# A hybrid encoder layer on one core: the delta rule's block inverses spread over two steps, and gate weights prepared in two parts

## The chip, the cores and the metric

The kernel runs on 1 core of one Trainium2 chip. The metric is the device time of one execution in microseconds (us), here the median of three runs.

## The reference, cut to what matters

One encoder layer: x + RMSNorm(W_out([A | B | M] * silu(z))), where the attention branch A, the delta-rule branch B, the memory branch M and the gates z all read one input projection of RMSNorm(x) (sequence 2048, width 1024). The change lies in branch B and in the projection of the gates.

```python
def gated_delta_rule_chunked(q, k, v, g, beta):      # per head and direction, chunks of 64
    ...
    lower = jnp.where(strict, jnp.einsum('...id,...jd->...ij', k_beta, k) * decay, 0.0)
    t_mat = lower + jnp.eye(CHUNK, dtype=lower.dtype)
    sol = lax.linalg.triangular_solve(t_mat, rhs, left_side=True, lower=True, unit_diagonal=True)
    ...
    def step(state, inp):
        qc, kc, uc, wc, ac, dc = inp
        v_new = uc - jnp.einsum('...cd,...de->...ce', wc, state)
        o = jnp.einsum('...cd,...de->...ce', qc, state) + jnp.einsum('...ij,...je->...ie', ac, v_new)
        state = state * dc[..., None, None] + jnp.einsum('...cd,...ce->...de', kc, v_new)
        return state, o
```

Four heads, forward and backward; the two directions are summed.

## The kernel before, in words

The kernel works on chunks of 128 tokens (16 of them, `TB`) and on two pairs of heads (`hp`); a step of the recurrence takes chunk s forward and chunk 15 - s backward for both heads of a pair, so there are 32 steps. TensorE (PE) runs the stage in the order in which the program writes it (`pin(T)`); VectorE (DVE), ScalarE (ACT), GpSimd (POOL) and the DMA queue of SyncE (SP) are ordered by a planner with a clock of its own, and each then serves its queue in that order.

Between the products of the delta rule the program puts gate products: `fill(n)` issues n products of 128x512 of `all_units`, which works through ten groups of 192 products (gates `z` and memory queries `mq`, 24 products to one output tile). There are 1920 of them in all; 48 come before the stage, 72 are kept for the attention's start (`START`), and a last `fill` issues what is left. `FILL` holds the numbers: entries 4 to 10 are those inside one step (18 in sum), entry 3 the ones between the parts of a head and between the parts of the last `finish`, entry 1 those of each chunk of the preparation (`s3a`), entry 2 those behind each of the two block inverses.

Each group needs its weights: `load_w` (L165) starts their DMA on POOL's queue, has ACT sum the squares (`wss`), DVE add them (`wsb`), PE sum over partitions (`norm_pow2`, L150), and then DVE, ACT and POOL make the scaled halves `wparts`. `all_units` calls it for the next group at the third output tile (k == 2) of a group.

The preparation writes, for each chunk, the matrices `NI` (products of `kq` with itself times decays), and then inverts the 32x32 diagonal blocks on DVE into `FT`. `inverse(hp, s)` builds the 128x128 inverse `F` of one chunk from them, in five parts with a `yield` between: part 0 loads `nt` (`n<-NI`) and `ft` and copies blocks to `F` and `Tb`; part 1 computes `zz` and its copy `zs`; part 2 `to` and `fo`, copied to `Tb` and `F`; part 3 `z2` and its copy `z2s`; part 4 `f2`, copied to `F`. In the trace `zz`, `fo`, `z2` and `f2` are one tile, `inv`, and `to` is `invt`.

`step` (L985) runs, on PE: `ks`, `qp`, then part 1 of the inverse of chunk s+1, 2 gate products, `tx` (with `F` of this chunk), 2 products, part 2, a part of the `finish` of the pair before, 6 products, `kv`, part 3, `av`, 6 products, part 4, 2 products. DVE makes `vn` from `tx` and the state `St` from `kv`; ACT makes `oo` from `qp`. The first chunk of each pair has its parts 0 to 3 run ahead of the pair's steps (the head), with 30 + 3 x 12 products between. `finish` scales, turns and gates the outputs of a pair, two chunks at a time; for the first pair it rides in the second's steps, for the second it runs at the end, with 12 products after each of its parts.

Working buffers of the stage: two `F`, one each of `Tb`, `nt`, `ft` and `oo`, two of `xx`; four PSUM buffers under the tag `tp`.

Of the kernel before, what the change touches and what calls it, by code (L numbers as in the profile page):

```python
# [11 lines left out]
F32 = mybir.dt.float32  # L12
# [20 lines left out]
LAG = 5  # L33
FILL = (72, 10, 216, 12, 0, 2, 2, 6, 0, 6, 2, 40, 0)


@with_exitstack
def hybrid_layer(ctx: ExitStack, tc: tile.TileContext, t: dict, out, dbg=None):
# [126 lines left out]
    def load_w(srcs, width, fac=(1.0,), fetch=None):  # L165


        n = wcount[0]
        wcount[0] += 1
# [14 lines left out]
        sb, y, e, sc = small("wsb", BF16), small("wy"), small("we", I32), small("wsc")  # L184
        V.tensor_tensor(sb, ss[0], ss[1], op=ALU.add)
        norm_pow2(f"{n}", sb, sc, y, e)
        cs = [small("wc1", bufs=2)] * (len(fac) - 1) + [small("wc0", pool=const)]
# [6 lines left out]
        G.tensor_tensor(parts[1][:, 1], raws[1], parts[1][:, 0], op=ALU.subtract)  # L194
        return [(w[:, 0], w[:, 1]) for w in parts], cs

# [63 lines left out]

    def load_group(segs, fetch=None, fac=(1.0,)):
# [6 lines left out]
        return load_w(src, sum(n for _, n in segs), fac, fetch)  # L268

    def tok_proj(ps, wg, tb):  # L270
# [265 lines left out]
    def z_load(pair):  # L536
        wg, (c, half) = load_group([(3600 + 256 * pair, 256)], fac=(1.0, 0.5))
        V.tensor_scalar(gate_cs[pair], c, vcs15 if pair < 4 else wd if pair < 6 else mvcs15, None, op0=ALU.mult)
        return wg, half

# [4 lines left out]
    with tc.tile_pool(name="s2", bufs=1) as p:  # L545
        wg, bcs, xbs, svs, kts_ = {0: nxt[0]}, {0: nxt[1]}, {}, {}, {}

        def b_proj(ch, b):
            g, u = ch // 2, ch % 2
            if u == 1 and b == 0:  # L550
                if g < 5:
                    wg[g + 1], bcs[g + 1] = load_group([(1536 + 256 * (g + 1), 256)])
                else:
                    wg[6] = z_load(4)
            if b == 0:
# [131 lines left out]
    def all_units():  # L687
# [3 lines left out]
        def load(kind, n):  # L691
            if kind == "z":
                return z_load(n)
            wg, (c,) = load_group([(3088 + 256 * n, 256)], fac=(SCALE * 2.0 ** 30,))
            V.tensor_scalar(mcs[:, 2 * n:2 * n + 2], c.to_broadcast([128, 2]), mkcs, None, op0=ALU.mult)
            return wg
# [222 lines left out]
    with tc.tile_pool(name="s3b", bufs=1) as p:  # L919
        Fb = [p.tile([128, 2, 2, 128], F32, tag=f"F{i}", name=f"F{i}") for i in range(2)]  # L920
        Tb = p.tile([128, 2, 64], F32, tag="T64", name="T64")
        for i in range(2):
            G.memset(Fb[i], 0.0)
        G.memset(Tb, 0.0)

# [5 lines left out]
        def inverse(hp, s):  # L931

            nm = f"{hp}_{s}"
# [16 lines left out]
            zz = ps[:, 0:64].rearrange("p (h i) -> p h i", h=2)  # L950
            fo = ps[:, 64:128].rearrange("p (h i) -> p h i", h=2)
            to = tp_ps(f"invt{nm}", (128, 2, 32))
            z2 = ps[:, 192:320].rearrange("p (h i) -> p h i", h=2)
            f2 = ps[:, 320:448].rearrange("p (h i) -> p h i", h=2)
# [30 lines left out]

        def step(hp, s, St, oss, inv, inv1, side):
            nm = f"{hp}_{s}"
            cc = (s, TB - 1 - s)
            sh = [128, 2, 2, 128]
            F = Fb[s % 2]  # L990
            xx = p.tile([128, 2, 4, 2, 128], F32, tag="xx", name=f"xx{nm}", bufs=2)
# [15 lines left out]
            fill(FILL[4])  # L1007
            oo = p.tile(sh, F32, tag="oo", name=f"oo{nm}")
            if s > 0:
# [13 lines left out]
            fill(FILL[6])  # L1023
            next(inv1, None)
            side()
# [19 lines left out]
            fill(FILL[9])  # L1045
            next(inv1, None)
            fill(FILL[10])
# [13 lines left out]
        def finish(hp, oss):  # L1061
# [6 lines left out]
            for c in range(0, TB, 2):  # L1068
                tags = ("oo", "vn") if hp and c % 4 else ("fi", "ga")
                oi = p.tile([128, 2, 2, 128], F32, tag=tags[0], name=f"fi{hp}_{c}")  # L1070
                ga = p.tile([128, 2, 256], F32, tag=tags[1], name=f"ga{hp}_{c}")
# [14 lines left out]
        done = iter(())  # L1086
        for hp in range(2):
            St = p.tile([128, 2, 2, 128], F32, tag="St", name=f"St{hp}")
            oss = p.tile([128, 2, TB], F32, tag="oss", name=f"oss{hp}", bufs=2)
            inv = inverse(hp, 0)  # L1090
            next(inv)
            fill(30)
            for _ in range(3):
                next(inv)
                fill(FILL[3])
            for s in range(TB):
                inv1 = inverse(hp, s + 1) if s + 1 < TB else iter(())
                next(inv1, None)
                step(hp, s, St, oss, inv, inv1, lambda: next(done, None))
                inv = inv1  # L1100
            done = finish(hp, oss)
        fill(24)
        for _ in done:
            fill(FILL[3])

# [451 lines left out]
```

## Time and profile before

| | |
|---|---|
| median of 3 runs | 2458.18 us (2453.1 to 2463.39) |
| the profiled execution | 2451.84 us |
| its span, first to last instruction | 2450.1 us |
| mean granted clock of TensorE | 0.987 |
| PE busy | 2320.4 us (95%) |
| DVE busy | 1652.8 us (67%) |
| ACT busy | 1302.7 us (53%) |
| POOL busy | 750.2 us (31%) |

Times in the profile count from the first instruction; a row of a list of waits names the engine that waited, what it was about to do, and after the arrow the engine and tile that it waited for. PE's matmuls are pipelined, so that a busy PE is not one at its peak. The preparation of the delta rule lies between about 650 and 900 us, the steps between about 905 and 1277, the last `finish` up to 1330.

### The profile page before, as it was taken

Reading aid. Unit: us, or ns where it says so; the run is one execution under the profiler, and the core shown is the slowest. Engines: PE = TensorE matmul, PEld = TensorE weight load, DVE = VectorE, ACT = ScalarE, POOL = GpSimd, SP = SyncE. Lnnn points to the kernel's source line nnn. Section 1 sums busy time; section 2 is a strip of 40 time slices with the busy share of each in tenths; the row PEclk is TensorE's granted clock in tenths of the full one; section 3 lists DMA queues with packets and bytes.
Section 4 is the critical chain, followed back from the end, with each engine's and each line's share of the span. In section 5 each row is a group of like instructions: output and inputs, shape, how many; then the busy total and the mean of one; then the engine's idle time right before and its main releaser. Section 6 shows DMA issues by size and latency. Waiting matters only on the chain.

```text
span 2450.1 us, 42346 instructions
## 1 busy us (share of the span) xinstructions
PE 2320.4 (95%) x15846; PEld 1463.9 (60%) x15846; DVE 1652.8 (67%) x3321; ACT 1302.7 (53%) x2516; POOL 750.2 (31%) x446
## 2 busy tenths in 40 slices
PE   6999999999999989999999999999999999899998
PEld 6888864455454446656664566666666666544443
DVE  7777659999658845545553777878887777355553
ACT  5634436544443135555553788888988878211110
POOL 2146432112112221121020444444555645122110
PEclk9999999999999999999999999999999999999999
DMA  6456555334477457767865999999999999676551
GB/s 224 142 133 148 122 120 179 115 108 124 132 247 240 115 171 208 226 196 231 241 211 177 226 234 242 240 244 236 247 240 236 239 227 222 195 249 195 183 166 67
DMA packets 942126, 471.59 MB, mean 192 GB/s; under 512 B 721952, under 2 KB 889440, under 8 KB 941664
## 3 DMA queue, kind: packets, MB, share of 16 engines
q1 hardware_dynamic: 929472, 425.88, 67.8%
q0 software_dynamic: 12448, 43.00, 5.2%
q8 instruction: 125, 2.05, 0.3%
q14 instruction: 81, 0.66, 0.1%
HBM read 207.59 MB, written 108.10 MB: 129 GB/s over the span
## 4 chain that ended last, share of the span: by engine, by line
PE 34%; DMA 10%; issue 4%; ACT 3%; POOL 2%; DVE 2%; SPq 0%; ACTq 0%; DVEq 0%; POOLq 0%
PE o L51 12%; PE sa L51 8%; PE pva L51 7%; DMA PT<-hla 5%; PE z L51 3%; POOL hla L51 2%; DMA xx<-bx 1%; DMA Od<-oo 1%; ACT Pa L51 1%; PE sm L51 1%; PE pvm L51 1%; ACT hla L51 0%; DMA wor<-in_w_out 0%; DVE hla L51 0%; PE o_last L51 0%
## 5 line engine op out<-in xcount | busy, mean ns | idle before, releaser
L51 PEld LDWEIGHTS <-wparts 128*128 128x128 f16 x3072 | 294.7, 99 | 327.6 <-issue 18.5
L51 POOL TENSOR_TENSOR hla<-Pa,hla 128x1281 f16<-128x1281 f32 x128 | 335.9, 2624 | 309.3 <-DVE hla L51 300.7
L51 DVE TENSOR_REDUCE mxa<-sa 128x1 f32<-128x1024 f32 x256 | 313.3, 1224 | 144.2 <-PE sa L51 143.9
L51 PE MATMUL sa<-K,qa 128*128 128x512 f16 x1536 | 375.3, 381 | 31.3 <-ACT Pa L51 29.3
L51 PE MATMUL pva<-PT,V 128*128 128x256 f16 x3072 | 376.4, 273 | 0.0
L51 PE MATMUL z<-hT,wparts 128*128 128x512 f16 x1536 | 373.4, 384 | 0.0
L51 PEld LDWEIGHTS <-V 128*128 128x128 f16 x3072 | 300.6, 98 | 84.9
L51 ACT ACTIVATE Pa<-sa,mxa,misc 128x1024 f32<-128x1024 f32 x256 | 305.9, 1198 | 57.4 <-DVE mxa L51 55.5
L51 PE MATMUL o<-wo,mhl 128*128 128x512 f16 x1416 | 308.8, 381 | 7.4 <-ACT mhl L51 4.9
L51 ACT CAST hla<-Pa 128x2048 f16<-128x2048 f32 x128 | 243.0, 1899 | 66.8 <-DMA PT<-hla 61.1
L51 PE MATMUL b<-hT,wparts 128*128 128x512 f16 x1152 | 258.2, 381 | 0.0
L51 PEld LDWEIGHTS <-mhl 128*128 128x128 f16 x1464 | 143.6, 98 | 182.4 <-ACT mhl L51 5.2
L51 PEld LDWEIGHTS <-qa 128*128 128x128 f16 x1536 | 150.6, 98 | 167.8 <-issue 39.0
L51 PEld LDWEIGHTS <-hT 128*128 128x128 f16 x2304 | 225.9, 98 | 40.0 <-DVE t L51 9.4
L51 PE MATMUL q<-wparts,hT 128*128 128x256 f16 x1920 | 213.6, 275 | 8.8 <-DVE t L51 8.8
L51 POOL TENSOR_SCALAR wraw<-wraw,wsc 128x1024 f32<-128x1024 f32 (+1 forms) x22 | 76.0, 3454 | 313.1 <-DVE wy L51 269.8
L51 DVE SCALAR_TENSOR_TENSOR y<-xb,convw,y 128x512 f32<-128x512 f32 x192 | 147.8, 782 | 2.0
L77 POOL DMA_DIRECT2D gate<-zg x64 | 35.6, 556 | 367.2 <-DVE zg L51 196.4
L51 ACT CAST mhl<-mr 128x2048 f16<-128x2048 f32 (+1 forms) x16 | 29.1, 1818 | 222.0 <-PE o L51 172.3
L51 DVE SCALAR_TENSOR_TENSOR hla<-Pa,hla 128x768 f16<-128x768 f32 x128 | 135.8, 1061 | 3.4 <-ACT hla L51 3.0
L51 POOL TENSOR_TENSOR mg<-mg 128x1536 f32<-128x1536 f32 (+1 forms) x16 | 55.0, 3437 | 236.1 <-DMA mg<-r 180.8
L51 DVE TENSOR_TENSOR mhl<-mr,mhl 128x2048 f16<-128x2048 f32 (+1 forms) x16 | 46.2, 2887 | 87.5 <-ACT mhl L51 87.5
(358 smaller groups left out, 3211.4 us busy)
## 6 DMA issues: line engine op xcount, KB each, us to landing
xx<-bx SPq DMA_DIRECT2D x64, 512.0 KB
wraw<-in_w_in POOLq DMA_DIRECT2D x42, 512.0 KB, 5.4
wor<-in_w_out SPq DMA_DIRECT2D x32, 512.0 KB
gate<-zg POOLq DMA_DIRECT2D x64, 256.0 KB, 3.9
NI<-nit SPq DMA_DIRECT2D x32, 512.0 KB
mr<-mix SPq DMA_DIRECT2D x13, 1024.0 KB
mg<-r SPq DMA_DIRECT2D x13, 768.0 KB
x<-in_x SPq DMA_DIRECT2D x16, 512.0 KB
```

The costliest lines, as they stand in the source:

```text
L51: ins = f(*args, **kw)
L77: nc.gpsimd.dma_start(to, of)
```

## The change

- The block inverses: part 0, 1 and 2 of chunk n+2 and parts 3 and 4 of chunk n+1 now run in step n. Part 1 comes where part 2 was (behind `tx`), part 2 where part 4 was (end of the step), part 3 where part 1 was (behind `qp`), part 4 where part 3 was (behind `kv`). Steps are counted through both pairs, so the second pair has no head of its own; the first head runs parts 0 to 2 for two chunks and part 3 for one.
- Buffers: three `F`, two `Tb`, two each of `nt`, `ft` and `oo`, three `kq`. The PSUM tiles of the inverse are five short ones in place of two.
- `FILL`: 2 products behind `ks` (were 0), 5 ahead of `tx` (were 2), 23 in a step (were 18); 6 between the parts of the head (were 12); 8 after each part of the last `finish` (new entry 13; were 12). The total of 1920 stays.
- Weights: `load_w` yields ahead of `norm_pow2`; `all_units` calls the first half at k == 1 and the second at k == 4. Earlier stages call both halves at once.

```diff
-FILL = (72, 10, 216, 12, 0, 2, 2, 6, 0, 6, 2, 40, 0)
+FILL = (72, 10, 216, 6, 2, 5, 2, 6, 0, 6, 2, 40, 0, 8)
...
         V.tensor_tensor(sb, ss[0], ss[1], op=ALU.add)
+        yield
         norm_pow2(f"{n}", sb, sc, y, e)
...
-                if k == 2 and not last:
-                    nxt = load(*plan[i + 1])
+                if k in (1, 4) and not last:
+                    if k == 1:
+                        steps = load(*plan[i + 1])
+                    nxt = next(steps)
...
-                kq = p.tile([128, 2, 2, 128], F32, tag="kq", name=f"kq{nm}", bufs=2)
+                kq = p.tile([128, 2, 2, 128], F32, tag="kq", name=f"kq{nm}", bufs=3)
...
-            F = Fb[s % 2]
-            nt = p.tile([128, 2, 2, 128], F32, tag="nt", name=f"n2{nm}")
-            ft = p.tile([128, 2, 2, 2, 32], F32, tag="ft", name=f"ft{nm}")
+            F, Tb = Fb[n % 3], Tbs[n % 2]
+            nt = p.tile([128, 2, 2, 128], F32, tag="nt", name=f"n2{nm}", bufs=2)
+            ft = p.tile([128, 2, 2, 2, 32], F32, tag="ft", name=f"ft{nm}", bufs=2)
...
-            ps = tp_ps(f"inv{nm}", (128, 512))
...
+            zz = tp_ps(f"invz{nm}", (128, 2, 32))
...
+            to, fo = tp_ps(f"invt{nm}", (128, 2, 32)), tp_ps(f"invf{nm}", (128, 2, 32))
...
+            z2 = tp_ps(f"invy{nm}", (128, 2, 64))
...
+            f2 = tp_ps(f"inv{nm}", (128, 2, 64))
...
-            oo = p.tile(sh, F32, tag="oo", name=f"oo{nm}")
+            oo = p.tile(sh, F32, tag="oo", name=f"oo{nm}", bufs=2)
...
             fill(FILL[6])
-            next(inv1, None)
+            next(inv2, None)
...
             fill(FILL[9])
-            next(inv1, None)
+            next(inv2, None)
...
+        order = [(hp, s) for hp in range(2) for s in range(TB)]
+        invs = [inverse(*x) for x in order]
+        for n in range(2):
+            next(invs[n])
+        fill(30)
+        for k in range(3):
+            for n in range(2 if k < 2 else 1):
+                next(invs[n])
+            fill(FILL[3])
+        invs += [iter(()), iter(())]
+        for n, (hp, s) in enumerate(order):
...
+            next(invs[n + 2], None)
+            step(hp, s, St, oss, *invs[n:n + 3], lambda: next(done, None))
+            if s == TB - 1:
+                done = finish(hp, oss)
         fill(24)
         for _ in done:
-            fill(FILL[3])
+            fill(FILL[13])
```

## Rows read from the trace of the kernel before

**Rows 1.** Stretches: window, its length, busy us per engine (count), PEclk, DMA share, GB/s

```profile
core 0: us, PE busy (x) PEld busy (x) DVE busy (x) ACT busy (x) POOL busy (x), PEclk, DMA share, GB/s
905.00:1277.00 372.00, 346.12 (x3658) 243.29 (x3657) 199.56 (x632) 206.35 (x786) 56.97 (x54) 1.00 0.72 217
1277.00:1330.00 53.00, 53.00 (x263) 26.15 (x262) 15.88 (x41) 17.14 (x49) 6.78 (x11) 1.00 0.57 183
```

**Rows 2.** PE's waits, 905 to 1277 us: total us, times, longest

```profile
PE inv L51 <- ACT F L51: 7.2, 9, 1.4
PE inv L51 <- ACT z2s L51: 6.4, 9, 2.0
PE inv L51 <- DMA n<-NI: 5.0, 5, 1.9
PE tx L51 <- DVE xx L51: 1.8, 3, 1.0
PE kv L51 <- DVE vn L51: 1.8, 4, 1.0
```

**Rows 3.** PE's waits over the whole span, the two of the preparation

```profile
PE pg L51 <- DMA kq<-bx: 8.2, 5, 3.2
PE wss L51 <- DVE wsb L51: 8.2, 2, 6.0
```

**Rows 4.** One step in order of time: start, us, engine, operation, count [idle before <- releaser]

```profile
1009.88 1.16 PE L51 MATMUL kv<-vn,xx 128*128 128x128 f32 x8
1010.11 1.14 ACT L51 ACTIVATE oo<-qp,gam 128x128 f32<-128x128 f32 x4 [3.30 <-DMA Od<-oo]
...
1011.13 0.83 ACT L51 COPY F<-inv 32x64 f32<-32x64 f32 x4
...
1012.02 0.45 PE L51 MATMUL inv<-T,n 64*64 64x64 f32 x8 [0.97 <-ACT F L51]
...
1013.39 1.46 PE L51 MATMUL z<-hT,wparts 128*128 128x512 f16 x6
...
1016.49 1.06 PE L51 MATMUL qp<-St,xx 128*128 128x128 f32 x8
...
1020.16 0.48 DVE L51 TENSOR_SCALAR xx<-xx,tail 128x128 f32<-128x128 f32 x2 [2.19 <-DMA xx<-bx]
```

**Rows 5.** The preparation in order of time: two loads of `kq` and a late product

```profile
701.46 0.64 SPq L51 DMA_DIRECT2D kq<-bx  x1
...
704.93 0.48 SPq L51 DMA_DIRECT2D kq<-bx  x1
...
710.18 2.04 PE L51 MATMUL pg<-kq 128*128 128x256 f32 x4 [3.12 <-DMA kq<-bx]
```

**Rows 6.** Stretches behind PE's three longest waits; the granted clock is the third-last column

```profile
712.00:730.00 18.00, 18.00 (x75) 9.24 (x74) 7.77 (x22) 6.50 (x22) 1.10 (x2) 0.89 0.63 209
868.00:880.00 12.00, 12.00 (x45) 4.88 (x44) 9.79 (x24) 2.06 (x2) 4.05 (x4) 0.79 0.58 140
1150.00:1200.00 50.00, 47.21 (x493) 34.39 (x492) 26.02 (x82) 25.97 (x99) 3.19 (x5) 0.97 0.78 240
```

**Rows 7.** The last `finish` in order of time

```profile
1292.50 5.34 PE L51 MATMUL z<-hT,wparts 128*128 128x512 f16 x24
...
1292.70 0.69 DVE L51 SCALAR_TENSOR_TENSOR ga<-ot,ga 128x512 f32<-128x512 f32 x1 [3.57 <-PE ot L51]
...
1293.42 0.36 SPq L51 DMA_DIRECT2D mix<-ga  x1
...
1296.81 0.36 SPq L51 DMA_DIRECT2D ga<-gate  x1
...
1298.32 0.69 DVE L51 SCALAR_TENSOR_TENSOR ga<-ot,ga 128x512 f32<-128x512 f32 x1 [4.33 <-PE ot L51]
```

**Rows 8.** Instructions on the tile `St`: duration min/median/max in ns

```profile
L51 DVE SCALAR_TENSOR_TENSOR St<-St,egl,kv x112: 337/342/349, 923.0 to 1268.6; 128x128 f32<-128x128 f32 x112
```

**Rows 9.** A gate weight during the block inverses, in order of time

```profile
818.31 0.18 PE L51 MATMUL wss<-wsb,onesb 128*128 128x1 bf16 x1 [2.12 <-DVE wsb L51]
...
834.83 2.22 POOL L51 TENSOR_TENSOR wparts<-wraw,wparts 128x1024 f16<-128x1024 f32 x1
```

More of the change, by code (lines that the diff above doesn't have):

```diff
@@ L194, in load_w @@
         G.tensor_tensor(parts[1][:, 1], raws[1], parts[1][:, 0], op=ALU.subtract)
-        return [(w[:, 0], w[:, 1]) for w in parts], cs
+        yield [(w[:, 0], w[:, 1]) for w in parts], cs
     p1 = ExitStack()
@@ L259, in hybrid_layer, with begin_group @@
     wpool = w12.enter_context(tc.tile_pool(name="w12", bufs=1))
-    def load_group(segs, fetch=None, fac=(1.0,)):
+    def begin_group(segs, fetch=None, fac=(1.0,)):
         def src(raw, half):
@@ L268, in load_group @@
         return load_w(src, sum(n for _, n in segs), fac, fetch)
+    def load_group(*args, **kw):
+        _, loaded = begin_group(*args, **kw)
+        return loaded
     def tok_proj(ps, wg, tb):
@@ L536, in z_load @@
     def z_load(pair):
-        wg, (c, half) = load_group([(3600 + 256 * pair, 256)], fac=(1.0, 0.5))
+        steps = begin_group([(3600 + 256 * pair, 256)], fac=(1.0, 0.5))
+        yield next(steps)
+        wg, (c, half) = next(steps)
         V.tensor_scalar(gate_cs[pair], c, vcs15 if pair < 4 else wd if pair < 6 else mvcs15, None, op0=ALU.mult)
-        return wg, half
+        yield wg, half
     def bx(hp, b, i, h):
@@ L553, in b_proj @@
                 else:
-                    wg[6] = z_load(4)
+                    _, wg[6] = z_load(4)
             if b == 0:
@@ L693, in load, with mq_load @@
                 return z_load(n)
-            wg, (c,) = load_group([(3088 + 256 * n, 256)], fac=(SCALE * 2.0 ** 30,))
+            return mq_load(n)
+        def mq_load(n):
+            steps = begin_group([(3088 + 256 * n, 256)], fac=(SCALE * 2.0 ** 30,))
+            yield next(steps)
+            wg, (c,) = next(steps)
             V.tensor_scalar(mcs[:, 2 * n:2 * n + 2], c.to_broadcast([128, 2]), mkcs, None, op0=ALU.mult)
-            return wg
+            yield wg
         nxt = first_z
@@ L919, in hybrid_layer @@
     with tc.tile_pool(name="s3b", bufs=1) as p:
[L920 to L924, printed above, removed]
+        Fb = [p.tile([128, 2, 2, 128], F32, tag=f"F{i}", name=f"F{i}") for i in range(3)]
+        Tbs = [p.tile([128, 2, 64], F32, tag=f"T64{i}", name=f"T64{i}") for i in range(2)]
+        for x in Fb + Tbs:
+            G.memset(x, 0.0)
         def blk(k):
@@ L931, in inverse @@
         def inverse(hp, s):
-            nm = f"{hp}_{s}"
-            F = Fb[s % 2]
-            nt = p.tile([128, 2, 2, 128], F32, tag="nt", name=f"n2{nm}")
-            ft = p.tile([128, 2, 2, 2, 32], F32, tag="ft", name=f"ft{nm}")
+            nm, n = f"{hp}_{s}", hp * TB + s
+            F, Tb = Fb[n % 3], Tbs[n % 2]
+            nt = p.tile([128, 2, 2, 128], F32, tag="nt", name=f"n2{nm}", bufs=2)
+            ft = p.tile([128, 2, 2, 2, 32], F32, tag="ft", name=f"ft{nm}", bufs=2)
             hs = slice(2 * hp, 2 * hp + 2)
@@ L948, in inverse @@
                 A.copy(Tb[blk(b), :, o:o + 32], tcp[blk(b), b // 2, :, :])
-            ps = tp_ps(f"inv{nm}", (128, 512))
[L950 to L954, printed above, removed]
             yield
+            zz = tp_ps(f"invz{nm}", (128, 2, 32))
             for h in range(2):
@@ L984, in inverse, with step @@
             V.tensor_copy(F[64:128, 1, :, 0:64], f2[64:128])
-        def step(hp, s, St, oss, inv, inv1, side):
+        def step(hp, s, St, oss, inv, inv1, inv2, side):
             nm = f"{hp}_{s}"
@@ L989, in step @@
             sh = [128, 2, 2, 128]
-            F = Fb[s % 2]
+            F = Fb[(hp * TB + s) % 3]
             xx = p.tile([128, 2, 4, 2, 128], F32, tag="xx", name=f"xx{nm}", bufs=2)
@@ L1069, in finish @@
                 tags = ("oo", "vn") if hp and c % 4 else ("fi", "ga")
-                oi = p.tile([128, 2, 2, 128], F32, tag=tags[0], name=f"fi{hp}_{c}")
+                oi = p.tile([128, 2, 2, 128], F32, tag=tags[0], name=f"fi{hp}_{c}", bufs=2 if tags[0] == "oo" else 1)
                 ga = p.tile([128, 2, 256], F32, tag=tags[1], name=f"ga{hp}_{c}")
@@ L1086, in hybrid_layer @@
         done = iter(())
[L1087 to L1094, printed above, removed]
-                fill(FILL[3])
[L1096 to L1101, printed above, removed]
+        order = [(hp, s) for hp in range(2) for s in range(TB)]
[9 more added lines that the diff above has]
+        for n, (hp, s) in enumerate(order):
+            if s == 0:
+                St = p.tile([128, 2, 2, 128], F32, tag="St", name=f"St{hp}")
+                oss = p.tile([128, 2, TB], F32, tag="oss", name=f"oss{hp}", bufs=2)
+            next(invs[n + 2], None)
+            step(hp, s, St, oss, *invs[n:n + 3], lambda: next(done, None))
+            if s == TB - 1:
+                done = finish(hp, oss)
         fill(24)
         for _ in done:
-            fill(FILL[3])
+            fill(FILL[13])
     fill(1920 - 24 * START - filled[0])
```

## The prediction, made before the change was built

> **What bounds the kernel now.** I read the stretches first: over the delta rule's recurrence, 905 to 1277 us, PE (TensorE) is busy 346.1 of 372 us, against 199.6 on DVE (VectorE) and 206.4 on ACT (ScalarE) [rows 1]. PE runs in the order of the program and every product of the stage stands in that order, so the stage lasts as long as PE's work plus PE's waits. The change adds no product and removes none. So it can only give back waits, and the second view is the list of what PE waited for. In the recurrence the waits ahead of products of `inverse` sum to 7.2 + 6.4 + 5.0 = 18.6 us in 23 places (single ones left out); the links of the recurrence itself (`tx`, `kv`) wait only 1.8 + 1.8 us in 7 places [rows 2]. Outside it two more waits lie where the diff touches: 8.2 us in 5 places for the loads `kq`, 8.2 us in 2 places for the sum of squares of a gate weight (`wsb`) [rows 3].
>
> The third view, one step in order of time, says where such a wait comes from. ACT stood idle 3.30 us ahead of `oo<-qp`, because the single `oo` buffer was still being stored (`Od<-oo`); the copies `F<-inv`, queued behind it on ACT, ran at 1011.13, and PE's `z2` product at 1012.02 had waited 0.97 us for them [rows 4]. So the wait of PE is short, and its cause is an engine that serves its queue in order and is held up by a DMA.
>
> **The clock's part.** The three longest waits are 3.1 us for `kq`, 6.0 us for `wsb` and 1.9 us for `n<-NI` [rows 2, 3, 5]; in the stretches behind them the granted clock reads 0.89 over 18 us, 0.79 over 12 us and 0.97 over 50 us [rows 6]; a share below 1 with levels of 1.2 and 2.4 GHz is time at the lower one. The work lost there is 0.11 x 18 + 0.21 x 12 + 0.03 x 50 = 6.0 us. Where the wait goes, this should go with it; I take 5 of 6, since a wait that only shrinks may still lower the clock.
>
> **A term that the list of waits hides.** A product counts as busy for longer than it holds PE back: 24 gate products take 5.34 us [rows 7] and 6 take 1.46 [rows 4], so one more costs (5.34 - 1.46) / 18 = 0.216 us, and the last one lasts 1.46 - 5 x 0.216 = 0.38 us. A wait that opens behind a product has swallowed 0.16 us before it shows. 30 waits (23 + 5 + 2) make 4.8 us; I take 4.3.
>
> **The change, part by part.**
>
> *Inverses over two steps.* A step now does for chunk n+2 the loads, the copies, `zz` and `to`/`fo`, and for n+1 `z2` and `f2`. The instructions are the same, so their own cost is nil; what changes is the distance from a result to its reader on PE. From `zs` to its readers PE had 2 products, `tx` and 2 products, 1.9 us; it now has 6 products, `kv`, `f2`, `av` and 6 products, about 1.30 + 1.16 + 0.45 + 1.16 + 1.30 = 5.4 us (`av` taken as `kv`, the same shape) [rows 4]. `z2s` goes from `av` and 6 products, 2.5 us, to 5 products, `tx`, 2 products, `zz`, 6 products and `kv`, over 5 us. The shortest one left is from `fo` to `z2`: 2 products, `ks`, 2 products, `qp`, 0.43 + 1.06 + 0.43 + 1.06 = 3.0 us (`ks` taken as `qp`, the same shape), against 6 products and `kv`, 2.5 us, today; the copies need 0.83 us on ACT [rows 4]. That gain of 0.5 us alone would not cover a 0.97 us wait, but the second `oo` buffer takes away the 3.30 us that held ACT up. `n<-NI` and `ft` get a second buffer, and `zz`, their first reader on PE, moves behind `tx`. The new PSUM tiles end one more bond, since `z2` no longer shares a tile with the `fo` that ACT is copying. I take 17 of 18.6 us; bounds 9 (half the waits stay, as ACT is still held up by DMAs) and 18.6.
>
> *Five more products per step.* 2 behind `ks`, 3 more ahead of `tx`, in 32 steps 160 x 0.216 = 34.6 us of work that comes in. It leaves elsewhere: the first head gives 66 - 48 = 18 products, the second head 66, the last `finish` 16 x 4 = 64, the rest after it 12; together 160. The sum on PE is nil. What hides behind them: from `ks` to `tx` the cover grows from 1.06 + 0.45 + 0.43 = 1.9 (the small products taken as those of `z2`) to 0.43 + 1.06 + 0.45 + 1.08 = 3.0 us, against four updates on DVE of 0.342 us or 1.4 us (taken from those of `St`, the same kind) [rows 4, 8]. From `tx` to `kv` it stays as it is, 2 products, small ones and 6 products, about 2.0 us. So `kv` and `tx` stay exposed to a DVE that is late because it waits for the DMA of `xx`, 2.19 us in one row [rows 4]: their 3.6 us stay, and as PE comes sooner to each link I add as much again, 4 us (bounds 0 and 8).
>
> *The pair of heads without a pause.* The head of the second pair is gone with its 66 products. It was hidden work; only its waits, which are in the 23, go. Its cost is nil.
>
> *The last `finish` with 8 products.* Today 24 products and four transposes make a pitch of 5.62 us (from one product of DVE on `ga`, 1292.70, to the next, 1298.32), and PE never waits [rows 1, 7]. With 16 it is 5.62 - 8 x 0.216 = 3.89 us. A `ga` buffer is stored at 1293.42 and its reload goes out at 1296.81, 3.39 us later [rows 7]; with as much for the reload and 0.69 us for the product on it, a buffer turns in about 7.5 us, and there are two, so 3.7 us per chunk pair: just under the 3.89. If SP's queue, which holds reload and store in one line, made each pair wait in series, 3.39 + 0.7 + 0.4 = 4.5 us would be the pitch and 8 x 0.6 = 5 us lost; the worst is the present pitch, 8 x 1.73 = 13.8 us. I take 2.
>
> *Gate weights in two steps.* `load_w` now stops ahead of the PE product of the sum of squares; it starts at product 24 of a group and goes on at 96, where both stood at 48. PE's wait there came from DVE, whose queue is full with the block inverses: `wsb` came 6.0 and 2.1 us late [rows 3, 9]. 48 products later are 10.4 us, more than either. So 8.2 us go; bounds 0 and 8.2. The weights must be ready at product 192, 96 x 0.216 = 20.7 us later: from the product at 818.31 to the end of the last POOL operation at 834.83 + 2.22 it took 18.7 us [rows 9]. That leaves 2 us of slack, and the first reader of that last part comes 3 us into the group. POOL's queue holds the next weight's DMA and the stores of gates behind it; they shift by the same 10 us and have 23 us until used. Cost nil; if the cover went, some 2 us once or twice.
>
> *A third `kq`.* A load was issued at 701.46 and its product had to wait until 710.18, 3.12 us late [rows 5]. A third buffer lets a load go out one iteration earlier, 3.47 us (the next one went out at 704.93). That covers the longest wait, barely; SP's queue, in which loads stand behind stores, can still hold one. 6.5 of 8.2 us; bounds 3 and 8.2.
>
> **The sum.** 17 + 8.2 + 6.5 = 31.7; hidden parts of the waits 4.3; clock 5; less 4 for the links, less 2 for `finish`: 35 us. The profiled execution took 2451.84 us (span 2450.1, 1.7 around it), so it would come to 2417; the median of the runs is 6.3 us above it, so 2458.2 - 35 = 2423 us.
>
> **The rivals.**
>
> *The waits move to the recurrence's links.* ACT and DVE still stand behind DMAs (`xx`, `ft`), and the denser PE meets that at `tx`, `kv` and `z2`. Then the inverses give 9 instead of 17, the links cost 8 instead of 4, and clock and hidden parts give 6 instead of 9.3; with `finish` unchanged 9 + 8.2 + 6.5 + 6 - 8 - 2 = 20 us, 2438. For it: the 2.19 us of DVE's wait; against: both engines are little over half busy [rows 1]. With 3 for `kq` and 5 lost in `finish`, 2445.
>
> *`finish` becomes bound by its DMAs.* 13.8 instead of 2: 2435.
>
> *PSUM runs short, the slower side.* Nine tiles per step instead of six go through the four `tp` buffers. `to` and `fo` can be held until DVE has read `kv`, that is updated `St`. The cover from `kv` is `f2`, `av` and 6 products, 2.9 us; DVE needs 1.4, so it decides where DVE starts more than 1.5 us late. If DVE were late in every step by the 3.2 us that its longest wait for `xx` would cost, 1.7 us x 31 = 53 us would be lost: 2423 + 53 = 2476. Against: no wait in the list is for a buffer, each is for a result, and a tile is now held for less time than the old one that lasted a whole step.
>
> The Trainium skill, page "Perfetto Trace Analysis", section "Optimization Strategy", says that bubbles repeating on the engine that should be saturated can mean too little SBUF or PSUM for the next tile. By that rule the change, which takes more PSUM tiles, would go this rival's way, to the 2476 worked out above. The rows name ACT's copies, `z2s` and a DMA as what ended the waits, so the trace bears the rule out for the SBUF buffer `oo` and not for PSUM.
>
> *It doesn't do what it says.* ACT, DVE, POOL and SP are ordered by a planner's own clock; if it orders the longer distances away, all stays within some 6 us of 2458.
>
> **How the numbers follow.** Forecast 0.62 (2423); links 0.16 (2438); `finish` 0.10 (2435); nothing happens 0.07 (2458); PSUM 0.05 (2476). The low end is all waits, hidden parts and the clock gone, 18.6 + 8.2 + 8.2 + 4.8 + 6 + 3.6 = 49 us: 2409, put at 2405 for the single waits left out. The high end takes in the links' bound, 2446. About 0.5%, or 12 us, is what a measurement of this kernel can tell from no change, so faster means under 2446: 0.62 + 0.10 + 0.12 of the links = 0.84; same 0.11; slower 0.05.
>
> **What would show it.** Right: in the list of PE's waits the rows `inv <- ACT F`, `ACT z2s`, `DMA n` go below 3 us together, `wss <- DVE wsb` is gone, `pg <- DMA kq` is under 2 us, the stretches after them read clock 1.00, and ACT's wait on `Od<-oo` is gone. Wrong: new rows `tx`, `kv`, `to` or `fo` <- DVE over 8 us in sum, `ot <- ACT fi` in the last `finish`, a wait of `z` or `mq` for `wparts`, or a stage behind 1330 us that grew by what the recurrence gave.

## The result and the profile after

The kernel after takes 2430.22 us in the median of six runs (2420.37 to 2437.66), the kernel before beside it 2455.64 us (2446.82 to 2463.39): a ratio of 0.9905 with an interval of 0.988 to 0.9929, some 25 us. The forecast was 35 us, 2423. The profiled execution was the fastest of the six (2420.37 us, span 2418.6); a second profile of the same kernel, `a_again` below, has a span of 2425.1 us, and I read both where a few us matter.

First the list of PE's waits over the whole span of the kernel after (total us, times, longest); of it the rows between the preparation and the attention:

```profile
PE z L51 <- POOL wparts L51: 4.7, 1, 4.7
PE pg L51 <- DMA kq<-bx: 4.1, 4, 1.8
PE invy L51 <- DVE T L51: 3.1, 3, 1.8
PE tx L51 <- DVE xx L51: 2.3, 5, 0.7
...
PE ot L51 <- ACT fi L51: 1.5, 1, 1.5
PE inv L51 <- ACT z2s L51: 1.4, 1, 1.4
...
PE invt L51 <- ACT zs L51: 1.2, 1, 1.2
```

Against [rows 2] the 18.6 us ahead of `inverse` are gone from the steps; `invy <- DVE T` (3.1) is new there, `tx` stands at 2.3 where it stood at 1.8, `kv` has no row. `inv <- z2s` and `invt <- zs` are both in the head. Against [rows 3] `pg` has halved and `wss` is gone, but `z <- POOL wparts`, 4.7 us at once, is new.

Then the stretches of the kernel after (window, length, busy us per engine, granted clock, DMA share, GB/s), which answer to [rows 1, 6]:

```profile
842.00:850.00 8.00, 3.32 (x9) 1.04 (x8) 2.41 (x5) 2.65 (x9) 6.00 (x9) 0.72 0.51 115
850.00:870.00 20.00, 20.00 (x89) 8.82 (x88) 16.79 (x38) 8.15 (x19) 1.95 (x4) 0.94 0.70 245
...
903.00:1257.00 354.00, 348.55 (x3585) 247.53 (x3585) 198.19 (x625) 199.04 (x754) 58.32 (x57) 1.00 0.73 225
```

In the steps PE is busy 348.6 of 354 us, where it was 346.1 of 372 [rows 1]; the clock's longest low stretch now lies behind the new 4.7 us wait (0.72, then 0.94).

To sum this up I cut both traces by PE's own products: preparation from the first `psg` up to the last `pg`, block inverses up to the first product of `inverse`, head up to the first `ks` (it holds the first step, which has no `ks`), steps up to the last `av`, last `finish` up to the attention's first `sa`. The cuts lie at 651.7, 782.1, 897.6, 915.9, 1276.7 and 1333.1 us before, and at 649.0, 774.0, 884.4, 902.7, 1257.3 and 1301.2 after. From the first `sa` on both need the same (1117.0 and 1117.4 us to the end of the span), so the whole gain is made ahead of it; 2.7 us of it in this one execution lie before the first cut, where nothing was changed. The gate products in the stages, counted in the traces, are 350, 472, 54, 616 and 236 before, and 350, 472, 41, 705 and 160 after; a product that moves takes its 0.216 us along, so "given back" below is the change in length plus 0.216 x the products that came in.

| us | preparation | block inverses | head | steps | last `finish` | sum |
|---|---|---|---|---|---|---|
| before | 130.4 | 115.5 | 18.3 | 360.8 | 56.4 | 681.4 |
| after | 125.0 | 110.4 | 18.4 | 354.6 | 43.8 | 652.2 |
| given back | 5.4 | 5.1 | -2.9 | 25.4 | -3.8 | 29.2 |
| second profile | 124.7 | 111.4 | 22.3 | 356.6 | 45.0 | 660.0 |
| given back | 5.7 | 4.1 | -6.8 | 23.4 | -5.0 | 21.4 |
| forecast | 8.9 | 10.6 | 0 | 17.5 | -2 | 35 |

(The last row is the prediction's sum by stages: `kq` 6.5 and `wss` 8.2 with their shares of the hidden parts and the clock, 17 - 4 with theirs for the steps.) The steps gave more than forecast; every stage around them gave less.

### The profile page after: what moved, and what is told of

The parts are those of the page before. It is cut to its first block, busy times and chain, and to the rows that moved or that the text cites. A ratio compares the mean times of both kernels' runs of the same rounds, so it can differ in the third digit from the quotient of the medians.

```text
span 2418.6 us, 42214 instructions
## 1 busy us (share of the span) xinstructions
PE 2309.8 (96%) x15838; PEld 1463.6 (61%) x15846; DVE 1647.2 (68%) x3321; ACT 1300.1 (54%) x2516; POOL 747.1 (31%) x448
## 4 chain that ended last, share of the span: by engine, by line
PE 60%; DMA 15%; DVE 9%; issue 6%; ACT 4%; POOL 3%; SPq 3%; DVEq 0%; ACTq 0%; POOLq 0%
PE o L51 12%; PE z L51 11%; PE sa L51 8%; PE pva L51 7%; PE q L51 6%; DMA PT<-hla 6%; PE b L51 5%; SPq L51 2%; DMA xx<-bx 2%; PE av L51 2%; POOL hla L51 2%; DMA wor<-in_w_out 2%; DVE y L51 1%; PE tx L51 1%; DMA NI<-nit 1%
## 5 line engine op out<-in xcount | busy, mean ns | idle before, releaser
L51 DVE SCALAR_TENSOR_TENSOR hla<-Pa,hla 128x768 f16<-128x768 f32 x128 | 128.5, 1004 | 2.3 <-ACT hla L51 2.3
```

Source lines behind the costliest of these rows:

```text
L51: ins = f(*args, **kw)
```

## The experiments

Each is one edit of the kernel before (`e_`) or after (`a_`), timed in five rounds beside the kernel before. Lengths of stages come from their own profiles, one execution each, by the cuts above. Such a length is only good to some us: the steps take 360.8, 363.6 and 369.2 us in the three kernels whose steps are those of the kernel before (it, `e_load`, `e_kq3`), and 354.6, 356.6 and 359.7 in three whose steps are those of the kernel after (it, `a_again`, `a_vset`).

| | median us | ratio to before, interval | preparation | block inverses | head | steps | `finish` |
|---|---|---|---|---|---|---|---|
| e_oo2 | 2450.63 | 1.0003 (0.9989 to 1.0017) | 129.9 | 113.7 | 18.2 | 357.9 | 57.7 |
| e_load | 2449.80 | 0.9997 (0.9982 to 1.0012) | 129.0 | 110.4 | 18.9 | 363.6 | 57.9 |
| e_kq3 | 2446.04 | 0.998 (0.9962 to 0.9998) | 124.0 | 113.7 | 18.2 | 369.2 | 56.9 |
| a_inv1 | 2435.77 | 0.9948 (0.9928 to 0.9967) | 123.8 | 110.3 | 20.9 | 365.8 | 44.4 |
| a_fill18 | 2447.35 | 1.0001 (0.9986 to 1.0016) | 124.6 | 110.4 | 18.7 | 346.1 | 79.0 |
| a_again | 2429.89 | 0.9915 (0.9902 to 0.9928) | 124.7 | 111.4 | 22.3 | 356.6 | 45.0 |
| a_xx3 | 2436.01 | 0.9943 (0.9931 to 0.9956) | 125.0 | 112.2 | 26.6 | 358.6 | 45.0 |
| a_dma | 2458.07 | 1.0037 (1.0024 to 1.005) | 124.1 | 111.8 | 44.2 | 361.0 | 44.1 |
| a_it2 | 2430.38 | 0.9917 (0.9896 to 0.9937) | 125.6 | 110.5 | 20.2 | 357.9 | 43.6 |
| f18_half | 2447.26 | 0.9983 (0.9967 to 0.9998) | 124.4 | 112.1 | 18.8 | 343.0 | 79.6 |
| a_vset | 2426.47 | 0.9907 (0.9888 to 0.9927) | 123.6 | 110.9 | 18.1 | 359.7 | 43.1 |
| a_bal | 2424.26 | 0.988 (0.9859 to 0.9901) | 124.8 | 108.2 | 18.6 | 360.6 | 44.2 |

### The second `oo` buffer alone

```diff
-            oo = p.tile(sh, F32, tag="oo", name=f"oo{nm}")
+            oo = p.tile(sh, F32, tag="oo", name=f"oo{nm}", bufs=2)
```

> The kernel before with one change: two `oo` buffers (and the same count where the last `finish` uses that tag). Theory 1, ACT's queue: the inverses waited because ACT stood behind the store of the single `oo`; then ACT's waits on `Od<-oo` (48 us in the recurrence) go, PE's waits ahead of products of `inverse` (18.6 us in 905 to 1277) fall to 8 us or less, and the time falls by 8 to 12 us. Theory 2, distance: each part of the inverse follows too soon on the one before, whatever ACT does; then those waits stay at 14 us or more and the time falls by 0 to 4 us.

1.0003: nothing. ACT's wait `oo <- Od<-oo` (48.3 us in the steps before) is gone, and another DMA stands in its place. Two of ACT's waits in the steps of the kernel before:

```profile
ACT oo L51 <- DMA Od<-oo: 48.3, 19, 4.2
...
ACT F L51 <- DMA ft<-FT: 20.3, 16, 2.8
```

ACT's waits in the steps, then PE's, of `e_oo2`:

```profile
ACT F L51 <- PE inv L51: 50.0, 38, 3.4
ACT F L51 <- DMA ft<-FT: 44.1, 26, 3.2
```

```profile
PE inv L51 <- ACT z2s L51: 7.4, 9, 1.6
PE inv L51 <- DMA n<-NI: 4.8, 5, 2.2
PE kv L51 <- DVE vn L51: 3.5, 5, 1.1
PE tx L51 <- DVE xx L51: 2.4, 3, 1.7
PE tx L51 <- ACT oo L51: 1.6, 3, 1.0
```

ACT waited 20.3 us for `ft` before and 44.1 now: it comes sooner to the next thing that is not there. PE loses its waits for `F` (7.2 to 0.7 us) and keeps those for `z2s` and `n`.

### The inverses back in one step

```diff
-            next(invs[n + 2], None)
-            step(hp, s, St, oss, *invs[n:n + 3], lambda: next(done, None))
+            next(invs[n + 1], None)
+            step(hp, s, St, oss, invs[n], invs[n + 1], invs[n + 1], lambda: next(done, None))
```

> The changed kernel with the inverses back in one step (parts 0 to 4 of chunk n+1 all in step n, one chunk in the head), everything else kept: buffers, PSUM tiles, five more products, weights in two steps, no pause between the pairs. Theory 1, ACT's queue: the spread is worth little, PE's waits ahead of the inverses' products come to 8 us or less in the steps, and the time is 22 to 28 us under the kernel before, as with the whole change (25.4). Theory 2, distance: these waits come back to 14 us or more, and the time is only 8 to 16 us under the kernel before.

On top of all the rest, the spread is worth 0.9948 against 0.9915, 8 us by the ratios and 6 by the medians (2435.8 against 2429.9), and the steps are 9.2 to 11.2 us longer than in the two profiles with it. PE's waits in the steps, then the first row of ACT's, of `a_inv1`:

```profile
PE inv L51 <- ACT z2s L51: 9.2, 10, 1.9
PE kv L51 <- DVE vn L51: 5.0, 4, 2.0
```

```profile
ACT F L51 <- DMA ft<-FT: 73.1, 27, 5.1
```

This is what the spread takes away. With the same buffers and the same 23 products, ACT stands 73.1 us behind the load of `ft` when the load is for the chunk of the next step; in the kernel after, where it is for the chunk after that, ACT has no wait on `ft` in the steps at all. `z2s`, queued behind it, is then in time.

### Eighteen products per step

```diff
-FILL = (72, 10, 216, 6, 2, 5, 2, 6, 0, 6, 2, 40, 0, 8)
+FILL = (72, 10, 216, 6, 0, 2, 2, 6, 0, 6, 2, 40, 0, 8)
```

> The changed kernel with 18 gate products in a step in place of 23 (0 behind `ks`, 2 ahead of `tx`); the 160 products left over come after the last `finish`. Forecast's theory, TensorE's work and its waits: the products cost the same there, and with 0.4 us and 0.65 us less cover the time is within 5 us of the changed kernel. Rival theory, feed of the steps: a step has a length of its own, set by how fast its loads come and DVE and ACT get at them, and products only fill it; then the steps become shorter by less than half of the 34.6 us that leave them, waits of `tx`, `kv` and the inverses come back with 15 us or more, and the time is 12 to 25 us above the changed kernel.

The gain is gone: 1.0001, with the spread, the buffers, the loads and the weights all in. The steps hold 66 products less than before, 14.3 us, and are 14.7 us shorter: the spread gave back 0.4 us here, and 3.5 us in `f18_half` below, whose steps have the same products (343.0 us). PE's waits in the steps of `a_fill18`, and their stretch:

```profile
PE tx L51 <- DVE xx L51: 11.7, 16, 1.7
PE invy L51 <- DVE T L51: 4.4, 4, 1.9
PE invy L51 <- ACT oi L51: 3.3, 1, 3.3
```

```profile
903.00:1257.00 354.00, 334.00 (x3501) 236.72 (x3496) 195.42 (x609) 197.34 (x757) 51.47 (x50) 0.98 0.73 225
```

The waits for ACT moved to `tx`, behind DVE, and the clock fell to 0.98 with them. DVE waits for the loads of `xx` in all of these kernels alike (75.6 us in the steps before, 66.0 after, 68.1 here); what differs is how many products PE has ahead of `tx` to cover it. The 160 products, 34.6 us, went to the last `finish` (79.0 against 43.8), where they cover nothing. Which of the two places does it, the 2 behind `ks` or the 3 ahead of `tx`, was not tried apart.

### The weights in two steps alone, and the third `kq` alone

```diff
-                if k == 2 and not last:
-                    nxt = load(*plan[i + 1])
+                if k in (1, 4) and not last:
+                    if k == 1:
+                        steps = load(*plan[i + 1])
+                    nxt = next(steps)
```

> The kernel before with gate weights in two steps alone. Forecast's step: both waits of `wss` for `wsb` (8.2 us) go and the clock's loss behind the longer one (2.5 us) with them: 9 to 12 us less. Rival, seen in the changed kernel: a wait of PE for `wparts` of some 5 us takes the place of one of them, since POOL's last operation on the weights stands behind the clearing of `F`: 3 to 6 us less. If the wait for `wparts` came from the third `F` and second `T` buffers, this kernel, which has neither, has no such wait.

```diff
-                kq = p.tile([128, 2, 2, 128], F32, tag="kq", name=f"kq{nm}", bufs=2)
+                kq = p.tile([128, 2, 2, 128], F32, tag="kq", name=f"kq{nm}", bufs=3)
```

> The kernel before with a third `kq` buffer alone. Forecast's step: 8.2 us of waits fall to under 2, and the clock's loss behind the 3.1 us wait (2.0 us) goes: 7 to 9 us less. Rival: the loads are late in SP's queue and in the DMA engines, not for want of a buffer; half of the waits stay, as in the changed kernel (4.1 us in 4 places), and the time falls by 3 to 6 us; if none of it came from the buffer, 0 to 2.

Each shortens the stage that it is in, by 5.1 and 6.4 us, and moves the time by nothing (0.9997) or by some 4 us (0.998): in both profiles the steps, which neither edit touches, came out longer, 363.6 and 369.2 against 360.8. Whether that is execution to execution or an effect of the earlier start I can't tell from one profile each; that of `e_kq3` is of an execution 4.4 us above its median. In `e_kq3` a wait of another kind opens in the preparation. In `e_load` PE has no wait for `wparts`, but one for DVE's `mqo`, ahead of a gate product. POOL clears `F` ahead of the weight's last operation here too, and that operation was done at 845.76, without a wait of PE for it; `mqo` was late because it stood on DVE behind operations on `xx`, which waited 6.11 and 2.43 us for their loads. PE in the preparation of `e_kq3`, PE in the block inverses of `e_load`, and DVE there:

```profile
PE pe L51 <- DVE nit L51: 2.5, 1, 2.5
PE pg L51 <- DMA kq<-bx: 1.0, 2, 0.7
```

```profile
PE z L51 <- DVE mqo L51: 5.7, 2, 3.5
```

```profile
849.57 0.48 DVE L51 TENSOR_SCALAR xx<-xx,tail 128x128 f32<-128x128 f32 x2 [6.11 <-DMA xx<-bx]
...
850.55 0.68 DVE L51 SCALAR_TENSOR_TENSOR mqo<-mq,mqo 128x512 f16<-128x512 f32 x1
```

### The clearing of `F` on DVE instead of POOL

The new wait for `wparts` in the kernel after, in order of time:

```profile
843.19 1.44 POOL L51 MEMSET F<- 128x512 f32 x3 [3.52 <-DMA FT<-rr]
...
844.58 0.34 POOL L51 MEMSET T<- 128x128 f32 x2
...
844.90 2.11 POOL L51 TENSOR_TENSOR wparts<-wraw,wparts 128x1024 f16<-128x1024 f32 x1
...
847.07 2.32 PE L51 MATMUL z<-hT,wparts 128*128 128x512 f16 x5 [4.68 <-POOL wparts L51]
847.23 0.50 ACT L51 COPY T<-ft 32x64 f32<-32x64 f32 x2 [8.83 <-DMA ft<-FT]
```

POOL stands 3.52 us behind the store of `FT`, because the clearing of `F` ahead of it waits for that; the last operation on the weight, ready by then, stands behind, and PE waits 4.68 us. In the kernel before the same clearing waited longer, and hurt nobody, since the weight's last operation had long been done (at 834.83 [rows 9]):

```profile
852.72 0.99 POOL L51 MEMSET F<- 128x512 f32 x2 [4.80 <-DMA FT<-rr]
```

```diff
         for x in Fb + Tbs:
-            G.memset(x, 0.0)
+            V.memset(x, 0.0)
```

> The changed kernel with the clearing of `F` and `T` on DVE in place of POOL. In the changed kernel POOL stood 3.5 us at that clearing, waiting for the store of `FT` to free the room, with the last operation on a gate weight behind it; PE then waited 4.7 us for `wparts`, and the clock read 0.72 over the 8 us and 0.94 over the 20 us behind it. If POOL's queue is the cause, that wait goes and the time falls by 4 to 7 us against the changed kernel (2429.9). If the weight was late because DVE stood behind the block inverses, the wait stays at 3 us or more; DVE may also hold up what stands behind the clearing on its own queue, which would show as new waits of the first inverse.

The `wparts` row goes, as the theory said, but no gain that is clear of the noise comes of it: 0.9907 (0.9888 to 0.9927) against 0.9915 (0.9902 to 0.9928), with 4 to 7 us expected and 3.4 us between the medians. PE's one wait there, then DVE's clearing and what comes behind it, in `a_vset`:

```profile
PE z L51 <- DVE mqo L51: 6.1, 1, 6.1
```

```profile
843.20 1.56 DVE L51 MEMSET F<- 128x512 f32 x3 [3.47 <-DMA FT<-rr]
...
849.50 0.50 ACT L51 COPY T<-ft 32x64 f32<-32x64 f32 x2 [10.61 <-DMA ft<-FT]
850.02 0.60 ACT L51 ACTIVATE mqo<-mq 128x512 f16<-128x512 f32 x1
...
850.65 0.69 DVE L51 SCALAR_TENSOR_TENSOR mqo<-mq,mqo 128x512 f16<-128x512 f32 x1 [3.61 <-ACT mqo L51]
```

Now DVE stands 3.47 us behind the same store, but that is not what PE waits for. DVE is done with the clearing at 845.04 and later stands idle 3.61 us ahead of its part of `mqo`, for ACT's part; ACT stood 10.61 us for the load of `ft`, with `mqo` queued behind it. In the kernel after ACT stood 8.83 us for the same load, up to 847.23, when `wparts` had just released PE (847.07). So there the wait for `wparts` covered a second one, and an edit that takes the first away leaves PE to the second.

### A third `xx` buffer

```diff
-            xx = p.tile([128, 2, 4, 2, 128], F32, tag="xx", name=f"xx{nm}", bufs=2)
+            xx = p.tile([128, 2, 4, 2, 128], F32, tag="xx", name=f"xx{nm}", bufs=3)
```

> The changed kernel with a third `xx` buffer, so that a step's keys, queries and values can be loaded a step earlier. If the steps are late because DVE stands behind these loads (68 us of DVE's waits on `xx <- DMA` in the changed kernel), that wait falls to a third or less, PE's waits `tx <- DVE xx` and `invy <- DVE T` (5.4 us) go, and the time falls by 5 to 10 us more. If the DMA engines' throughput is what limits, the loads come no sooner and the time stays within 3 us of the changed kernel.

It is 6 us slower than the kernel after beside it, and DVE's wait for `xx` in the steps is what it was, 68.8 us (66.0 and 74.4 in the two profiles without the edit). So the number of buffers isn't what holds the loads. Its longest new wait is in the head, which is 4.3 us longer than in `a_again`; PE there, and SP's queue, of `a_xx3`:

```profile
PE invf L51 <- DVE T L51: 7.2, 1, 7.2
```

```profile
882.54 2.40 SPq L51 DMA_DIRECT2D xx<-bx  x4
885.07 0.58 SPq L51 DMA_DIRECT2D ga<-gate  x1
886.02 9.94 SPq L51 DMA_DIRECT2D ft<-FT  x8
```

Loads of `xx`, these four and two just before them, go out ahead of the `ft` of the third and fourth chunk, which take 9.94 us to issue (4.04 us in the kernel after), and ACT stands 7.8 us for the first of these. PE's 7.2 us end a little earlier, with DVE's copy of `invt` into `T` at 896.63: it stands on DVE behind the operations on `xx` of the first steps, each of which waited 0.3 to 1.8 us for its load, and behind two on `zg`. `invf` reads nothing that DVE wrote, so this may have been a wait for the PSUM buffer that the copy frees; that is not shown.

### More bytes, fewer bytes

```diff
-            it = p.tile(sh, F32, tag="it", name=f"it{nm}")
+            wide = p.tile([128, 2, 2, 2, 128], F32, tag="it", name=f"it{nm}")
+            it = wide[:, :, 1]
...
-                dma(it[:, d], NI_d[hp, d, cc[d], :, 1])
+                dma(wide[:, d], NI_d[hp, d, cc[d]])
```

> The changed kernel with the loads of `it` doubled: the same instructions on SP, the same waits, in the same places of the steps, but 128 KB more in each of the two loads of a step (256 KB a step, 8.2 MB in 32 steps, a tenth more than the 79.6 MB that the steps move). Theory, bytes: the steps are limited by what the DMA engines deliver (223 to 225 GB/s there); a step grows by about 256 KB / 224 GB/s = 1.17 us, and the time by 25 to 37 us, as waits of `tx` for DVE's `xx` and of the inverses, spread over the steps. Rival, order: the steps are limited by SP's queue or by DVE and ACT standing behind single loads; bytes are free, and the time grows by 0 to 8 us.

`f18_half`, on top of `a_fill18`, with one `it` tile made ahead of the steps:

```diff
-                dma(it[:, d], NI_d[hp, d, cc[d], :, 1])
+                n = 2 if s == 0 else 1
+                dma(it[:, d, 0:n], NI_d[hp, d, cc[d], :, 1, 0:n])
```

> The changed kernel with 18 gate products in a step (a_fill18, 2447 us), and with half of each load of `it` left out from the second step of a pair on, so that part of the products with `it` use old values: the same number of loads, 128 KB less in a step (4.0 MB in all, a twentieth). Theory, bytes: a step shortens by up to 128 KB / 224 GB/s = 0.57 us, the time falls by 10 to 18 us from a_fill18, to 2429 to 2437. Rival, order: within 4 us of a_fill18.

`a_dma`, on top of the kernel after:

```diff
+            extra = p.tile(sh, F32, tag="extra", name=f"extra{nm}", bufs=2)
+            dma(extra, bx_d[hp, s, :, 0:2])
```

> The changed kernel with one more load of 256 KB in each of the 32 steps, into a buffer that nothing reads (8.4 MB more, about a tenth of the 79.5 MB that the steps move). If the steps are limited by the DMA engines' throughput (225 GB/s in the steps of the changed kernel), each step grows by 256 KB / 225 GB/s = 1.2 us and the time by 25 to 40 us. If there is room (the engines were busy 0.73 of the time), the time grows by 0 to 8 us, by longer latencies only.

`a_it2` moves 256 KB more in each step by the same instructions, and takes 2430.38 us against the 2429.89 of the kernel after. Its steps:

```profile
911.00:1268.00 357.00, 347.81 (x3582) 246.15 (x3582) 197.57 (x625) 198.99 (x753) 58.35 (x57) 1.00 0.78 245
```

245 GB/s instead of 225, at no cost. `f18_half` is `a_fill18` with half of each `it` load left out from the second step on, and gives back 0 to 4 us where the bytes would have given 10 to 18: 2447.26 against 2447.35 by the medians, 0.9983 against 1.0001 by the ratios, and PE's row `tx <- DVE xx` still has 10.2 us in 14 places (11.7 in 16 without the edit). So the bytes don't set the time of the steps. Both edits change the size of packets and hardly their number, so that a limit by the number of packets is not ruled out. `a_dma` was meant to ask the same with one more load per step and doesn't answer it: the planner put all the extra loads ahead of the steps, and its 28 us are in the main one wait in the head, where ACT and behind it PE stand 25.8 us for the `ft` of the third chunk:

```profile
PE inv L51 <- ACT z2s L51: 25.8, 1, 25.8
```

### The 23 products laid out anew

```diff
-FILL = (72, 10, 216, 6, 2, 5, 2, 6, 0, 6, 2, 40, 0, 8)
+FILL = (72, 10, 216, 6, 2, 6, 2, 5, 0, 4, 4, 40, 0, 8)
```

> The kernel after with the same 23 products per step, laid out anew: 6 instead of 5 ahead of tx, 5 instead of 6 ahead of kv, 4 + 4 instead of 6 + 2 in the two places around the last part of the inverse. Theory (a step's waits go where the cover behind a DMA-bound DVE or ACT is thin: ahead of tx, and between fo and z2): the waits tx <- DVE xx (4.2 us in 8 places in the second execution of the kernel after) and invy <- DVE T (2.8 us in 2) halve or better, kv <- DVE vn stays under 2 us, and the time comes 3 to 6 us below the kernel after (2429.9 us beside it in an earlier comparison), ratio to the kernel before about 0.989 to 0.990. Rival (where the products stand no longer matters once there are 23 in a step: the DMA under way sets the end): the same sum of waits within 2 us, spread otherwise, with kv as a new row, and a time within 3 us of the kernel after.

The time speaks for the theory (2424.26 us, ratio 0.988), the trace against it. PE's waits in the steps of `a_bal`:

```profile
PE tx L51 <- DVE xx L51: 5.8, 7, 2.1
PE kv L51 <- DVE vn L51: 4.2, 4, 1.3
```

The sum is no smaller (10.0 against 7.0 in `a_again`), `kv` is the new row that the rival expected, and the steps are 4 us longer. The profiled execution was the slowest of its five (2435.87; the other four are within 2422.9 to 2424.4), so the trace may not show what made the others short. But 10 us of that lie behind the first `sa` (1127.5 us against 1117.4), where the edit changes nothing, so that slowness does not excuse the steps. And the kernel after did not run on the same chip beside it; the interval of `a_bal` (0.9859 to 0.9901) overlaps that of the first comparison of the kernel after (0.988 to 0.9929). It stays open whether this layout is better. `a_again`, for the record, is the kernel after unchanged:

> The changed kernel once more, on the chip of the three runs beside it, as their anchor and for a second profile. The forecast (waits of TensorE's order, 35 us) would have it 30 us or more under the kernel before; the first measurement has it at 25.4 (17 to 30). If its profiled execution, 2420.4, was a lucky one, this one shows where a typical execution loses the other 10 us: the forecast's rival of the links says rows of `tx`, `kv` and DVE's `xx <- DMA` in the steps, the others say another stage.

## Why the prediction was right, and where it was not

**The sum.** 25 us lie inside the range, but in part by luck, since errors offset each other: in the first profile the steps gave 7.9 us more than forecast and the four stages around them 13.7 less, in the second 5.9 more and 19.5 less. Of the signs, `ACT F`, `ACT z2s` and `DMA n` are gone from PE's waits in the steps, `wss` is gone and so is ACT's `Od<-oo`; `pg` stayed at 4.1 us, over the 2 named. Two signs of being wrong came, `ot <- ACT fi` (1.5 us) and `z` for `wparts` (4.7 us).

**What bounds it.** PE's waits do set the stage. Where the waits fell the stage fell, and where they only moved (`a_fill18`, `e_oo2`) the time stood still.

**Inverses over two steps: right in sign, but only together with the five products.** With them the steps gave back 25.4 and 23.4 us, against 17.5 forecast. The reason was half right. I put the waits down to the short distance on PE and to ACT held up by `oo`; the second buffer for `oo` alone gave nothing, and ACT then stood behind `ft` (44.1 us). What the spread does is to ask for `ft` a whole step sooner: 73.1 us of ACT's wait without it, none with it.

**Five more products per step: the step that failed.** "The sum on PE is nil" holds, as 160 products cost 34.6 us wherever they stand (`a_fill18`: `finish` +35.2). But I let them hide nothing of weight and charged the links 4 us. Without them the spread gives back 0.4 us in the steps (3.5 in `f18_half`); without the spread, the 89 products that came in, 19.2 us, leave the steps of `a_inv1` only 5.0 us longer, so they hide 14.2; together it is 23 to 25. The cover from `ks` to `tx`, which I had counted as 1.9 to 3.0 us, is what keeps DVE's waits of 2 to 4 us for `xx` off PE:

```profile
1064.37 0.59 PE L51 MATMUL z<-hT,wparts 128*128 128x512 f16 x2
...
1064.81 1.05 PE L51 MATMUL qp<-St,xx 128*128 128x128 f32 x8
...
1065.76 0.29 DVE L51 TENSOR_SCALAR xx<-xx,tail 128x128 f32<-128x128 f32 x1 [3.28 <-DMA xx<-bx]
...
1066.08 0.47 DVE L51 COPY T<-invt 32x64 f32<-32x64 f32 x2
...
1066.35 0.69 PE L51 MATMUL invy<-T,n 64*64 64x64 f32 x8 [0.49 <-DVE T L51]
...
1066.98 1.25 PE L51 MATMUL z<-hT,wparts 128*128 128x512 f16 x5
```

In this step of the kernel after DVE stood 3.28 us for `xx`; of that 0.49 us reached PE, at `invy`, whose `T` is copied behind it on DVE. Ahead of `tx` stand the five products. So the links themselves cost nothing (`tx` 2.3, no `kv`) where I took 4; counted with `invy`, which waits for the same DVE, they have 5.4 and 7.0 us in the two profiles, against 3.6 before, and the rival "the waits move to the links" is what happens as soon as the cover is taken away, in full: its bound of 8 us was too small, as the whole gain goes.

**The head: left out.** "Its cost is nil" is true of the second pair's. The first now builds parts of two inverses with 6 products between in place of 12, and PE waits there for `zs` and `z2s`, 2.6 us (3.9 in the second profile). By the products that left it should be 2.8 us shorter; it is 0.1 to 4.0 us longer.

**Gate weights: right about `wss`, wrong about the rest.** The 8.2 us of waits went, 4.7 came back. "Cost nil", with 2 us of slack, failed: I looked along POOL's queue for DMAs and stores that shift, and not for what the weight's last operation would now stand behind. It moved from 834.83 to 844.90, past the clearing of `F`. That names the row, and not all of the cost: with the clearing off POOL's queue (`a_vset`) the stage still took 110.9 us, as `mqo` stood behind ACT's wait for `ft`. The stage gave 5.1 and 4.1 us of 10.6; in `a_bal`, where PE waited only 3.4 us for `wparts`, it gave 7.3.

**A third `kq`.** 4.1 of 8.2 us went (6.5 forecast, bounds 3 and 8.2), and alone (`e_kq3`) 7.2. With the clock the stage gave 5.4 of 8.9.

**The clock.** Over the preparation it reads 1.00 where it read 0.97. Over the block inverses it reads 0.97 where it read 0.96: the new wait left 0.72 and 0.94 behind it. In the steps the first profile won nothing, since the 50 us from 1050 on, around a wait of 1.8 us for `T`, read 0.97 as 50 us did before [rows 6]:

```profile
1050.00:1100.00 50.00, 47.73 (x496) 32.57 (x495) 25.84 (x82) 29.92 (x117) 5.46 (x6) 0.97 0.72 216
```

The second reads 1.00 in the steps, but 0.85 over the head and 0.96 over the last `finish`, where both read 1.00 before. The mean is 0.990 in the first profile and 0.987, as before, in the second: of my 5 us, all to about none. I had also not taken the three longest waits: [rows 3] has 3.2 us for `kq` and [rows 2] 2.0 us for `z2s`, and the clock read 1.00 behind both (741 to 760 and 1235 to 1250), while it read 0.89 over 815 to 830, around the 2.12 us of [rows 9]. So the length of a wait alone did not tell what it cost in clock.

**`finish`.** 2 us forecast, 3.8 and 5.0 lost. DVE's products on `ga` now come every 4.93 us (1271.47 to 1296.11 in five) where I had 3.89, 4.5 if SP's queue worked in series; the group over that stage names the load:

```profile
L51 DVE SCALAR_TENSOR_TENSOR ga<-ot,ga 128x512 f32<-128x512 f32 x8 | 5.5, 692 | 18.0 <-DMA ga<-gate 14.5 <-PE ot L51 3.4
```

DVE stands 14.5 us for the reload of `ga`, where it waited for PE before [rows 7]. Little of that reaches PE, which can run ahead of DVE: it shows 1.5 us ahead of `ot`, for ACT's `fi`, whose load goes out on the same queue, and 1.8 us ahead of the first `sa` (1.5 before). That the queue of SP costs all of the 3.8 us is not shown.

**PSUM.** No wait for `to` or `fo` on a buffer exists in the steps, so that rival is out there; the one wait that may be of its kind is in the head of `a_xx3`. The Trainium skill, page "Perfetto Trace Analysis", section "Optimization Strategy", says that consistent bubbles can mean that SBUF or PSUM does not suffice for the next tile. Here a second `oo` alone gave 1.0003 and a third `xx` 0.9943 against 0.9915, so that neither buffer alone helped: behind both stood a load.

**What stays open.** Why the loads of `xx` come late. Neither the bytes of `it` nor a third buffer moved DVE's wait for them far: it is 66.0 and 74.4 us in the two profiles of the kernel after, 77.2 in `a_it2` and 68.8 in `a_xx3`. In the head the order of SP's queue decides when `ft` comes (`a_xx3`, `a_dma`); for the steps that was not tried.

## What to carry to other kernels

A pause of an engine that runs in program order is hidden by distance on both sides: ask for the data sooner (the spread took ACT's 73.1 us for `ft`) and put filler ahead of the reader whose engine stands behind a load (the five products); either alone gave little or half. Filler that is moved is not neutral because its sum is: count what it covers where it arrives, and where it came from. When an operation is moved on an engine's queue, read what it will stand behind there, above all a cheap one that waits for a store; and before taking a wait away, look for the next one behind it on the other engines.

## What the runs showed of the hardware

- The steps took 245 GB/s as well as 225 (2430.38 against 2429.89 us), at a DMA share of 0.78 against 0.73. I had held the DMA engines to be what DVE waited for.
- Clearing a buffer on POOL, 0.99 to 1.44 us of work, waited 3.5 to 4.8 us for the store of `FT`; moved to DVE it waited as long, 3.47 us.
- One wait of 4.7 us on PE left the granted clock at 0.72 over the 8 us around it and at 0.94 over the next 20, so that part of them ran at 1.2 GHz.
